# Fourteen up-projection chunks by seven products, the gated product on GpSimd, and another order of sums and lows

## The chip, the cores and the metric

One core of a Trainium2 chip runs the kernel. The metric is the time of one execution in microseconds (us); the figure of a kernel is the median of several runs.

## The reference, cut to what matters

Two transformer layers over a sequence of 512 tokens with 1024 features, in float32. Each layer has an attention part and a gated feed-forward part with a short convolution in it. The change touches only the feed-forward part, and in it the up-projection:

```python
D_MODEL, SEQ, D_FF, CONV_W = 1024, 512, 2816, 3

def conv_ffn(xn, w_up, cw, cb, w_down):
    a = xn @ w_up                                   # (512, 1024) x (1024, 5632)
    ap = jnp.pad(a, ((0, 0), (CONV_W - 1, 0), (0, 0)))
    a = sum(ap[:, j:j + T] * cw[j] for j in range(CONV_W)) + cb
    gate, val = jnp.split(a, 2, axis=-1)
    return (jax.nn.gelu(gate, approximate=True) * val) @ w_down
...
for l in range(2):
    h = h + rms_norm(mix, g[1])                     # mix: the layer's attention
    f = conv_ffn(rms_norm(h, g[2]), w_up[l], conv_w[l], conv_b[l], w_down[l])
    h = h + rms_norm(f, g[3])
```

## The kernel before

**Precision.** Every float32 operand is split into a high part (its value rounded to the matmul's float32r format) and a low part (the rest). A product of two operands is three matmuls: high by high, high by low, low by high (`mm3`, lines 276 to 279). So each weight needs a high, which ScalarE makes with a copy, and a low. A low is made in one of two ways: VectorE subtracts the high from the raw weight, or ScalarE writes the negated high (`scale=-1.0`) and a DMA from GpSimd's queue adds the raw weight to it (`accum_op=ALU.add`).

**Chunks.** The 5632 columns of the up-projection are computed in 22 chunks per layer. Chunk c holds 128 columns of the gate (bank 0 of PSUM) and 128 columns of the value (bank 1), transposed: 128 features by 512 tokens. A chunk takes one of two ways:

- A *plain* chunk: for each of the two banks, 8 blocks of the 1024 features, 3 matmuls each of 512 tokens: 48 matmuls.
- A chunk *by seven products* (Strassen's scheme in Winograd's form; the chunks in the tuple `SEVEN`): the features are halved, the tokens are halved, the two banks are the other pair of halves. Seven products of 4 blocks by 3 matmuls of 256 tokens: 84 matmuls. The seven are named in the code by their weights, A11, S2, S3, A12, S1, A22, S4. The weights' sums S1 to S4 are computed anew for each chunk; the sums of the inputs are there from the start (`XA`, `XB`).

**Order of a chunk by seven.** TensorE runs A11, S2, S3, A12, S1, A22, S4. A11 of the next chunk is opened ahead of S4 of this one (`open_seven`), and ScalarE copies its sum aside (line 1015, `s1`). The results go to quarters of the two banks: `o1` (A11 and A12) and `o2` (S2, S1, S4) share bank 0, `o3` (S3, A22) and `o4` share bank 1. Between the products VectorE makes short sums of 256 columns: `s12` (line 995, behind S2), `s17` (996, behind S3), `o4` (1012), `o3` (1020), and last `o2` (1022, behind S4).

**The work on a finished chunk** is done while the next chunk runs. `taps` does the convolution: ScalarE scales the bank into `bb` (641), VectorE adds the two other taps (642, 644), for the gate and the value. `glu` is ScalarE's GELU (662). `product`, called one chunk later, sends the previous gated product to memory by a DMA from GpSimd's queue (`hD`, 657) and multiplies gate and value (`hc`, 659). The down-projection reads `hD`.

**The weights ahead.** The program order is written out by hand: every engine runs its instructions in the order in which the code names them, and the framework adds the waits. `prepare(c, part)` is called three times in chunk c and drives three generators through `step`, for the chunks c + 1 and c + 2:

- `first_weights` takes the two raw blocks (A11 with A12, A21 with A22), makes high and low of A11 and A12 (706 to 708, low by an adding DMA), S3 and S2 (`sa`, 709 and 711) with `a21 + a22` (710) on the way, their high (712) and low (716), and the sum S4 (714).
- `other_weights` makes high and low of S1 and S4 (725, 728) and of A22 (726, 729).
- `plain_weights` makes highs and lows of a plain chunk, for all but the last two chunks with adding DMAs (`high_added`, lines 53 to 88).

The raw weights come from HBM by SyncE's queue. All of this shares 16 large, 10 middle and 8 small buffers in SBUF and the 8 banks of PSUM.

Of the kernel before, what the change touches and what calls it, by code (L numbers as in the profile page):

```python
# [9 lines left out]
F32 = mybir.dt.float32  # L10
# [14 lines left out]
BIG = 3.0e38  # L25


SEVEN = (5, 6, 8, 9, 11, 12, 14, 15, 17, 18)
ND = NF // 2
LAST = 3  # L30
FILL = 26
# [70 lines left out]
def trunk_kernel(ctx, tc, x, norm_gains, w_qkv_a, w_o_a, w_q_b, w_o_b, kv_norm, w_kvf, b_f,  # L102
# [11 lines left out]
    def t8(shape, dt=F32, name="t8"):  # L114
        return p8.tile(shape, dt, tag="t8", name=name)
# [516 lines left out]
    def ffn(l, bd, cp, nxt, ahead):  # L632
# [19 lines left out]
        def product():  # L652

            if gated:
                c, bb = gated.pop()
                if c - 1 in hc:
                    pool.dma_start(hD[c - 1], hc.pop(c - 1))
                hc[c] = t2([128, T], name="hc")
                dve.tensor_tensor(hc[c], bb[:, 0, :], bb[:, 1, :], ALU.mult)

        def glu(c, bb):
            act.activation(bb[:, 0, :], bb[:, 0, :], AF.Gelu_apprx_tanh)
# [37 lines left out]
        def first_weights(c):  # L700

            r0, r1 = W.take(2)
            w0, w1 = (t8([128, 2, 1024], F32R, name="w") for _ in range(2))
            sa, sb = (t4([128, 1024], name="wsum") for _ in range(2))
            a11, a12, a21, a22 = r0[:, 0:512], r0[:, 512:1024], r1[:, 0:512], r1[:, 512:1024]
            act.copy(w0[:, 0], r0)
            act.activation(w0[:, 1], r0, AF.Copy, scale=-1.0)
            pool.dma_start(w0[:, 1], r0, accum_op=ALU.add)
            dve.tensor_tensor(sa[:, 0:512], a11, a21, ALU.subtract)
            dve.tensor_tensor(sb[:, 0:512], a21, a22, ALU.add)  # L710
            dve.tensor_tensor(sa[:, 512:1024], sb[:, 0:512], a11, ALU.subtract)
            act.copy(w1[:, 0], sa)
            yield
            dve.tensor_tensor(sb[:, 512:1024], a12, sa[:, 512:1024], ALU.subtract)
            yield
            dve.tensor_tensor(w1[:, 1], sa, w1[:, 0].bitcast(F32), ALU.subtract)
            half_way[c] = a22, sb
            v = [t.rearrange("p s (q k c) -> p s q k c", q=2, k=4) for t in (w0, w1)]
            halves[c] = dict(A11=v[0][:, :, 0], A12=v[0][:, :, 1], S3=v[1][:, :, 0], S2=v[1][:, :, 1])

        def other_weights(c):

            a22, sb = half_way.pop(c)
            w2, w3 = (t8([128, 2, 1024], F32R, name="w") for _ in range(2))
            act.copy(w2[:, 0], sb)
            act.copy(w3[:, 0, 0:512], a22)
            yield
            dve.tensor_tensor(w2[:, 1], sb, w2[:, 0].bitcast(F32), ALU.subtract)
            dve.tensor_tensor(w3[:, 1, 0:512], a22, w3[:, 0, 0:512].bitcast(F32), ALU.subtract)
            v = [t.rearrange("p s (q k c) -> p s q k c", q=2, k=4) for t in (w2, w3)]  # L730
            halves[c].update(S1=v[0][:, :, 0], S4=v[0][:, :, 1], A22=v[1][:, :, 0])

# [19 lines left out]
        def prepare(c, part):  # L752

            m, n = c + 1, c + 2
            if n >= NF:
                return
            after = c not in SEVEN
            if m in SEVEN:
                if part == 0 and not after:
                    step(1, m)  # L760
                if part == (0 if after else 1) or part == (1 if after else 2):
                    step(2, m)
            if n not in SEVEN:
                step(0, n)
                if part == 0 and n < NF - 2:
                    step(0, n)
            elif part < 2 or m not in SEVEN:
                step(1, n)

        acts, one, two, raws, later2 = {}, {}, {}, {}, {}  # L770
        H = slice(0, 512), slice(512, 1024)
# [196 lines left out]
        def prod(o, w, x, start=False):  # L968
            half_mm(o, w, x[0:2], x[2], start)
# [6 lines left out]
        for c in range(2, NF):  # L976
# [5 lines left out]
            if c in SEVEN:  # L982
                x21, x22 = [(xT[0][i], xT[1][i], s) for i, s in ((1, LO), (1, HI))]
                banks, s1 = opened or open_seven(c)
                was_open = opened is not None
                opened = None
                w = halves.pop(c)
                W.n_get += 2
                o1, o2, o3, o4 = banks[0][:, LO], banks[0][:, HI], banks[1][:, LO], banks[1][:, HI]
                s12, s17 = (t2([128, 256], name="csum") for _ in range(2))  # L990

                def two_sums():
                    if not was_open:
                        act.copy(s1, o1)
                    dve.tensor_tensor(s12, o2, s1, ALU.add)
                    dve.tensor_tensor(s17, o3, s1, ALU.add)

                prod(o2, w["S2"], (*XB, HI))
                prod(o3, w["S3"], (*XA, HI), True)
                product()  # L1000
                if was_open:
                    two_sums()
                    bb = taps(*before)
                else:
                    bb = taps(*before, two_sums)
                prepare(c, 0)
                glu(before[0], bb)
                prod(o1, w["A12"], x21)
                prod(o2, w["S1"], (*XA, LO))
                prod(o3, w["A22"], (*XB, LO))  # L1010
                prepare(c, 1)
                dve.tensor_tensor(o4, o2, s17, ALU.add)
                if c + 1 in SEVEN:
                    opened = open_seven(c + 1)
                    act.copy(opened[1], opened[0][0][:, LO])
                else:
                    begun = W.get(), bank([128, T], name="up")
                    up(*begun, range(4))
                prod(o2, w["S4"], x22)
                dve.tensor_tensor(o3, o3, s12, ALU.add)  # L1020
                prepare(c, 2)
                dve.tensor_tensor(o2, o2, s1, ALU.add)  # L1022
            else:
                banks = [bank([128, T], name="up") for _ in range(2)]
                for s in range(2):
                    if s == 0 and begun:
                        w, banks[0] = begun
                        up(*begun, range(4, KD))
                        begun = None
                    else:  # L1030
                        up(W.get(), banks[s], range(KD))
                    if c == NF - 2:
                        next(sums)
                    if s == 0 and before:
                        post(*before, (lambda: pair_lows(0)) if c == NF - 1 else None)
                        if c >= NF - 2:
                            pair_highs(c - NF + 2)
                            pair_sums(c - NF + 3)
                    if s == 0:
                        prepare(c, 0)  # L1040
                    prepare(c, 1 + s)
                    next(extra, None)
# [866 lines left out]
```

## Time and profile before

| | before |
|---|---|
| median of 3 runs | 1109.95 us (1109.84 to 1110.57) |
| the profiled execution | 1110.27 us, of it span 1108.5 |
| TensorE busy | 1098.4 us (99%) |
| VectorE busy | 896.6 us (81%) |
| ScalarE busy | 660.2 us (60%) |
| GpSimd busy | 222.2 us (20%) |
| TensorE's granted clock in the stretch 238 to 384 us | 1.00 |

In the rows of the profile PE is TensorE (PEld its weight loads), DVE VectorE, ACT ScalarE, POOL GpSimd, SP SyncE; L709 is line 709. A timeline's row has start and duration in us, engine, line, operation, the tiles written and read, and in brackets how long the engine stood idle before and for whom. Tile `up` is a PSUM bank of the up-projection, `wraw` a raw weight, `w` a split one, `wsum` holds sums of weights, `csum` the short sums. The chunks 5 to 18 of the two layers lie at about 238 to 384 us and 821 to 967 us; in the first of these, VectorE is busy 115 of 146 us.

### The profile page before, as it was taken

Reading aid. Unit: us, or ns where it says so; the run is one execution under the profiler, and the core shown is the slowest. Engines: PE = TensorE matmul, PEld = TensorE weight load, DVE = VectorE, ACT = ScalarE, POOL = GpSimd, SP = SyncE. Lnnn points to the kernel's source line nnn. Section 1 sums busy time; section 2 is a strip of 40 time slices with the busy share of each in tenths; the row PEclk is TensorE's granted clock in tenths of the full one; section 3 lists DMA queues with packets and bytes.
Section 4 is the critical chain, followed back from the end, with each engine's and each line's share of the span. In section 5 each row is a group of like instructions: output and inputs, shape, how many; then the busy total and the mean of one; then the engine's idle time right before and its main releaser. Section 6 shows DMA issues by size and latency. Waiting matters only on the chain.

```text
span 1108.5 us, 18139 instructions
## 1 busy us (share of the span) xinstructions
PE 1098.4 (99%) x6611; PEld 948.4 (86%) x6611; DVE 896.6 (81%) x1494; ACT 660.2 (60%) x1092; POOL 222.2 (20%) x329
## 2 busy tenths in 40 slices
PE   9999999999999999999999999999999999999997
PEld 6988889889999988888888787789989999988886
DVE  6577878978887799997877777858978887799995
ACT  5444566566565547476555677756565565547473
POOL 1832100211111111000010766600211111111000
PEclk9999999999999999999999999999999999999999
DMA  9469864467789989885872677584467779999872
GB/s 325 149 207 408 346 171 132 108 134 196 176 201 216 256 318 341 295 310 108 210 153 76 193 222 211 161 246 124 114 133 191 181 200 219 249 315 340 306 247 77
DMA packets 184563, 237.32 MB, mean 214 GB/s; under 512 B 11737, under 2 KB 131529, under 8 KB 183962
## 3 DMA queue, kind: packets, MB, share of 16 engines
q1 hardware_dynamic: 166970, 176.61, 49.0%
q0 software_dynamic: 17504, 59.55, 23.3%
q8 instruction: 52, 0.85, 0.3%
q14 instruction: 37, 0.30, 0.1%
HBM read 170.28 MB, written 39.63 MB: 189 GB/s over the span
## 4 chain that ended last, share of the span: by engine, by line
PE 89%; DVE 3%; issue 3%; ACT 2%; DMA 2%; POOL 1%; DVEq 0%; POOLq 0%; ACTq 0%
PE up L278 13%; PE up L277 13%; PE up L279 13%; PE acc L278 8%; PE acc L277 8%; PE acc L279 8%; PE qk_ps L278 2%; PE qk_ps L277 2%; PE qk_ps L279 2%; PE first L279 1%; PE first L277 1%; PE first L278 1%; PE o_ps L1762 1%; PE pT_ps L1747 1%; PE v_ps L278 1%
## 5 line engine op out<-in xcount | busy, mean ns | idle before, releaser
L277 PE MATMUL acc<-w 128*128 128x512 f32 (+1 forms) x311 | 120.5, 388 | 0.0
L279 PE MATMUL acc<-w 128*128 128x512 f32 (+1 forms) x311 | 120.4, 387 | 0.0
L57 ACT CAST w<-wraw 128x1024 fp32r<-128x1024 f32 x96 | 99.0, 1048 | 9.5 <-issue 3.9
L278 PE MATMUL acc<-w 128*128 128x512 f32 (+1 forms) x267 | 103.2, 387 | 0.0
L65 DVE TENSOR_TENSOR w<-wraw,w 128x1024 fp32r<-128x1024 f32 x66 | 88.1, 1356 | 15.1 <-ACT w L57 14.7
L641 ACT ACTIVATE bb<-up,conv 128x512 f32<-128x512 f32 x80 | 60.0, 776 | 67.3 <-DVE up L1022 42.8
L278 PE MATMUL up<-xbl,w 128*128 128x512 f32 (+1 forms) x280 | 96.3, 344 | 0.0
L278 PE MATMUL up<-xcl,w 128*128 128x512 f32 (+1 forms) x280 | 96.3, 344 | 0.0
L277 PE MATMUL up<-xch,w 128*128 128x512 f32 (+1 forms) x280 | 96.3, 344 | 0.0
L277 PE MATMUL up<-xbh,w 128*128 128x512 f32 (+1 forms) x280 | 96.3, 344 | 0.0
L279 PE MATMUL up<-xbh,w 128*128 128x512 f32 (+1 forms) x280 | 96.2, 344 | 0.0
L279 PE MATMUL up<-xch,w 128*128 128x512 f32 (+1 forms) x280 | 96.2, 344 | 0.0
L277 PE MATMUL up<-xsh,w 128*128 128x256 f32 x320 | 90.6, 283 | 0.0
L278 PE MATMUL up<-xsl,w 128*128 128x256 f32 x320 | 90.6, 283 | 0.0
L279 PE MATMUL up<-xsh,w 128*128 128x256 f32 x320 | 90.6, 283 | 0.0
L277 PEld LDWEIGHTS acc<-w 128*128 128x128 f32 x311 | 58.4, 188 | 12.0
L279 PEld LDWEIGHTS acc<-w 128*128 128x128 f32 x311 | 58.4, 188 | 11.8
L644 DVE SCALAR_TENSOR_TENSOR bb<-up,conv,bb 128x510 f32<-128x510 f32 x80 | 59.9, 749 | 2.8
L642 DVE SCALAR_TENSOR_TENSOR bb<-up,conv,bb 128x511 f32<-128x511 f32 x80 | 59.4, 742 | 2.6 <-ACT bb L641 2.6
L277 PEld LDWEIGHTS up<-xsh,w 128*128 128x128 f32 x320 | 61.4, 192 | 0.0
L278 PEld LDWEIGHTS up<-xsl,w 128*128 128x128 f32 x320 | 61.4, 192 | 0.0
L279 PEld LDWEIGHTS up<-xsh,w 128*128 128x128 f32 x320 | 61.4, 192 | 0.0
(337 smaller groups left out, 3161.2 us busy)
## 6 DMA issues: line engine op xcount, KB each, us to landing
wraw<-in_w_up_dram SPq DMA_DIRECT2D x88, 512.0 KB, 5.0
w<-wraw POOLq DMA_DIRECT2D x50, 512.0 KB, 6.1
dT<-dsums SPq DMA_DIRECT2D x24, 512.0 KB, 6.0
hD<-hc POOLq DMA_DIRECT2D x44, 256.0 KB, 7.6
dact<-hD SPq DMA_DIRECT2D x44, 256.0 KB, 5.2
wraw<-dT SPq DMA_DIRECT2D x22, 512.0 KB, 6.6
wraw<-in_w_down_dram SPq DMA_DIRECT2D x22, 512.0 KB
dsums<-in_w_down_dram SPq DMA_DIRECT2D x18, 512.0 KB, 5.6
```

The lines of the kernel that those rows point to most:

```text
L57: self.nc.scalar.copy(pair[:, 0], raw)
L65: self.nc.vector.tensor_tensor(pair[:, 1], raw, pair[:, 0].bitcast(F32), ALU.subtract)
L277: pe.matmul(o, ah, bh, start=first, stop=False, skip_group_check=shared)
L278: pe.matmul(o, ah, bl, start=False, stop=False, skip_group_check=shared)
L279: pe.matmul(o, al, bh, start=False, stop=last, skip_group_check=shared)
L641: act.activation(bb[:, s, :], ps, AF.Identity, bias=cp[:, 3, ch:ch + 1], scale=cp[:, 2, ch:ch + 1])
L642: dve.scalar_tensor_tensor(bb[:, s, 1:], ps[:, :T - 1], cp[:, 1, ch:ch + 1], bb[:, s, 1:], ALU.mult, ALU.add)
L644: dve.scalar_tensor_tensor(bb[:, s, 2:], ps[:, :T - 2], cp[:, 0, ch:ch + 1], bb[:, s, 2:], ALU.mult, ALU.add)
L1747: pe.transpose(o[:, k0 + k, :], p[:, hh, k * 128:(k + 1) * 128], ident)
L1762: pe.matmul(o[64 * hh:64 * hh + 64, i * 128:(i + 1) * 128], Vt[hd // 8][:, k, (hd % 8) * 64:(hd % 8) * 64 + 64], pT[j, i, hh][:, k, :], st ...
```

## The change

In both layers:

1. `SEVEN` takes in chunks 7, 10, 13 and 16. Before, one plain chunk stood between each two by seven products; after, chunks 5 to 18 all go by seven products. Chunks 0 to 4 and 19 to 21 stay plain.
2. The gated product (line 659) moves from VectorE to GpSimd, which also issues the DMA of `hD` ahead of it. This holds for all 22 chunks.
3. The low of A22 (line 729, on VectorE) is made by ScalarE's negated copy and an adding DMA in GpSimd's queue, at the head of `other_weights`.
4. The order of sums and lows changes: the first weight sum (709) for chunk c + 2 goes between the two short sums 995 and 996; the low of S3 and S2 (716) of chunk c + 1 goes ahead of them; 710 goes behind the taps, 711 and 714 behind `o4` (1012), which goes ahead of `prepare(c, 1)`. The low of S1 and S4 (728) stays ahead of the last sum (1022).

```diff
-SEVEN = (5, 6, 8, 9, 11, 12, 14, 15, 17, 18)
+SEVEN = (5,6,7,8,9,10,11,12,13,14,15,16,17,18)
...
                 hc[c] = t2([128, T], name="hc")
-                dve.tensor_tensor(hc[c], bb[:, 0, :], bb[:, 1, :], ALU.mult)
+                pool.tensor_tensor(hc[c], bb[:, 0, :], bb[:, 1, :], ALU.mult)
...
             a11, a12, a21, a22 = r0[:, 0:512], r0[:, 512:1024], r1[:, 0:512], r1[:, 512:1024]
+            dve.tensor_tensor(sa[:, 0:512], a11, a21, ALU.subtract)
+            yield
             act.copy(w0[:, 0], r0)
             act.activation(w0[:, 1], r0, AF.Copy, scale=-1.0)
             pool.dma_start(w0[:, 1], r0, accum_op=ALU.add)
-            dve.tensor_tensor(sa[:, 0:512], a11, a21, ALU.subtract)
             dve.tensor_tensor(sb[:, 0:512], a21, a22, ALU.add)
+            yield
             dve.tensor_tensor(sa[:, 512:1024], sb[:, 0:512], a11, ALU.subtract)
             act.copy(w1[:, 0], sa)
-            yield
             dve.tensor_tensor(sb[:, 512:1024], a12, sa[:, 512:1024], ALU.subtract)
             yield
...
             w2, w3 = (t8([128, 2, 1024], F32R, name="w") for _ in range(2))
+            act.copy(w3[:, 0, 0:512], a22)
+            act.activation(w3[:, 1, 0:512], a22, AF.Copy, scale=-1.0)
+            pool.dma_start(w3[:, 1, 0:512], a22, accum_op=ALU.add)
+            yield
             act.copy(w2[:, 0], sb)
-            act.copy(w3[:, 0, 0:512], a22)
             yield
             dve.tensor_tensor(w2[:, 1], sb, w2[:, 0].bitcast(F32), ALU.subtract)
-            dve.tensor_tensor(w3[:, 1, 0:512], a22, w3[:, 0, 0:512].bitcast(F32), ALU.subtract)
...
             if m in SEVEN:
-                if part == 0 and not after:
-                    step(1, m)
-                if part == (0 if after else 1) or part == (1 if after else 2):
-                    step(2, m)
+                step(2, m)
...
-            elif part < 2 or m not in SEVEN:
+            elif part < 2 or after or m not in SEVEN:
                 step(1, n)
+                if after and part == 0:
+                    step(1, n)
...
                     dve.tensor_tensor(s12, o2, s1, ALU.add)
+                    if c + 2 in SEVEN:
+                        step(1, c + 2)
                     dve.tensor_tensor(s17, o3, s1, ALU.add)
...
                 product()
+                if c + 1 in SEVEN:
+                    step(1, c + 1)
...
                 prod(o3, w["A22"], (*XB, LO))
+                dve.tensor_tensor(o4, o2, s17, ALU.add)
                 prepare(c, 1)
-                dve.tensor_tensor(o4, o2, s17, ALU.add)
```

## The prediction

> **What bounds the kernel now.** I read the page first: the busy shares, then the chain that ended last.
>
> ```profile
> span 1108.5 us, 18139 instructions
> PE 1098.4 (99%) x6611; PEld 948.4 (86%) x6611; DVE 896.6 (81%) x1494; ACT 660.2 (60%) x1092; POOL 222.2 (20%) x329
> PE 89%; DVE 3%; issue 3%; ACT 2%; DMA 2%; POOL 1%; DVEq 0%; POOLq 0%; ACTq 0%
> ```
>
> TensorE is busy 99% of the span and carries 89% of the chain: time is won only where matmuls go and lost only where a matmul waits. The profiled execution took 1110.27 us (1.8 of it outside the span); the median of the runs, 1109.95, is 0.3 less. Next the timeline of TensorE in the first layer's up-projections (columns: start, duration, engine).
>
> ```profile
> 227.28 0.39 PE L277 MATMUL up<-xbh,w 128*128 128x512 f32 x1
> 238.16 0.28 PE L277 MATMUL up<-xbh,w 128*128 128x256 f32 x1
> 246.79 0.28 PE L277 MATMUL up<-xbh,w 128*128 128x256 f32 x1
> 248.23 0.28 PE L277 MATMUL up<-xbh,w 128*128 128x256 f32 x1
> ```
>
> Durations overlap, so I take distances between starts. From 227.28 to 238.16 lie the 48 matmuls of a plain chunk: 10.88 us. From 238.16 to 248.23 lie seven products of 12 matmuls: 10.07, or 1.44 each. Product A22 of chunk 5 ends at 246.79, A11 of chunk 6 at 248.23; TensorE waits nowhere in between. The other engines in chunks 5 to 8:
>
> ```profile
> 246.99 0.43 DVE L1012 TENSOR_TENSOR up<-up,csum 128x256 f32<-128x256 f32 x1 [1.32 <-PE up L279]
> 247.80 1.22 DVE L728 TENSOR_TENSOR w<-wsum,w 128x1024 fp32r<-128x1024 f32 x1
> 248.93 0.69 DVE L729 TENSOR_TENSOR w<-wraw,w 128x512 fp32r<-128x512 f32 x1
> 249.87 0.43 DVE L1022 TENSOR_TENSOR up<-up,csum 128x256 f32<-128x256 f32 x1 [0.26 <-PE up L279]
> 250.21 0.68 DVE L659 TENSOR_TENSOR hc<-bb 128x512 f32<-128x512 f32 x1
> 253.09 0.74 DVE L642 SCALAR_TENSOR_TENSOR bb<-up,conv,bb 128x511 f32<-128x511 f32 x1
> 255.98 0.68 DVE L709 TENSOR_TENSOR wsum<-wraw 128x512 f32<-128x512 f32 x1
> 256.57 0.68 DVE L710 TENSOR_TENSOR wsum<-wraw 128x512 f32<-128x512 f32 x1
> 257.29 0.69 DVE L711 TENSOR_TENSOR wsum<-wsum,wraw 128x512 f32<-128x512 f32 x1
> 258.02 0.69 DVE L714 TENSOR_TENSOR wsum<-wraw,wsum 128x512 f32<-128x512 f32 x1
> 258.63 0.43 DVE L1012 TENSOR_TENSOR up<-up,csum 128x256 f32<-128x256 f32 x1
> 248.43 0.37 ACT L1015 COPY csum<-up 128x256 f32<-128x256 f32 x1 [0.39 <-PE up L279]
> 250.34 1.45 ACT L641 ACTIVATE bb<-up,conv 128x512 f32<-128x512 f32 x2 [1.54 <-DVE up L1022]
> 251.68 1.04 ACT L706 CAST w<-wraw 128x1024 fp32r<-128x1024 f32 x1
> 252.62 1.06 ACT L707 ACTIVATE w<-wraw 128x1024 fp32r<-128x1024 f32 x1
> 258.07 1.06 ACT L712 CAST w<-wsum 128x1024 fp32r<-128x1024 f32 x1 [4.40 <-DVE wsum L711]
> 259.03 0.63 ACT L662 ACTIVATE bb<-bb 128x512 f32<-128x512 f32 x1
> 265.63 0.61 ACT L726 CAST w<-wraw 128x512 fp32r<-128x512 f32 x1
> 266.15 1.05 ACT L706 CAST w<-wraw 128x1024 fp32r<-128x1024 f32 x1
> 253.97 0.84 POOL L708 DMA_DIRECT2D w<-wraw  x1 [6.18 <-ACT w L707]
> 254.51 0.87 POOL L657 DMA_DIRECT2D hD<-hc  x1
> ```
>
> What to see: L1012 writes the high half of a bank and starts 0.20 after A22 has finished with its low half (246.79), though S1, which it reads, ended 1.44 before; a bank is handed over whole. VectorE's distances are 0.60 for 512 columns (0.72 where the next needs the result), 1.13 for 1024 (247.80 to 248.93), 0.34 for 256 (249.87 to 250.21), 2.89 for four taps (253.09 to 255.98).
>
> **The change part by part.** *Chunks 7, 10, 13, 16 by seven products:* in two layers this takes 8 x (10.88 - 10.07) = 6.5 us from TensorE, and that is all that can be won.
>
> *Product to GpSimd, low of A22 to a DMA.* A chunk by seven products costs VectorE 2.89 for taps, 1.70 for five short sums, 2.66 for four weight sums (0.60 + 0.72 + 0.73 + 0.61), 2.26 for two lows, and now also 0.60 for the product and 0.60 for A22's low: 10.7, over the 10.07 of TensorE. Where plain chunks stand between, this averages out; 14 in a row without the two removals would lose 0.6 each. With them 9.5 is left. ScalarE gains a pass of 512 columns, 0.52 (265.63 to 266.15), and stays near 7 us; GpSimd has three DMA issues and a product, about 3 us. The new DMA is issued a chunk ahead of A22; its landing is hidden by 10 us of matmuls. By busy time everything fits.
>
> *By order it is tighter.* GpSimd's product is a new neighbour of VectorE's two-input instructions. The nearest rows, and the rows that time the hand-overs:
>
> ```profile
> 192.26 4.62 POOL L676 TENSOR_TENSOR xsum<-xbh,xbl 128x2048 f32<-128x2048 f32 x1 [52.06 <-DVE xbl L349]
> 192.92 5.04 DVE L65 TENSOR_TENSOR w<-wraw,w 128x1024 fp32r<-128x1024 f32 x1
> 24.17 0.46 POOL L1093 TENSOR_TENSOR tu<-qk,rope 128x128 f32<-128x128 f32 x1 [21.99 <-ACT qk L1087]
> 638.93 0.90 POOL L82 DMA_DIRECT2D w<-wraw  x1 [1.41 <-ACT w L59]
> 639.54 1.15 POOL L1696 TENSOR_SCALAR bias<-ck,cq 128x128 f32<-128x128 f32 x2
> L708 POOLq EVENT_SEMAPHORE  x38: 17/43/5618, 213.7 to 930.2; - x38
> 527.42 0.59 ACT L1414 COPY vp<-v_ps 128x512 f32<-128x512 f32 x1
> 528.06 0.19 PEld L277 LDWEIGHTS v_ps<-w,xkh 128*128 128x128 f32 x1 [0.56 <-ACT vp L1414]
> ```
>
> L65 takes 1.22 at its size (as L728), here 5.04: it stood still until 192.92 + 5.04 - 1.22 = 196.74, 0.14 before L676 ended at 196.88. So a GpSimd instruction with two SBUF inputs shuts out a VectorE instruction that also has two. A product of 512 columns lies between L1093 and L676: 0.46 + 384 x (4.62 - 0.46)/1920 = 1.29, and it shuts VectorE out for 1.15. Sums and lows (L709 to L728) are of the kind that is shut out; the short sums and taps read PSUM.
>
> When does the product run? Its place in GpSimd's queue is behind the two added DMAs of the chunk before. Follow one ring, from the sum that ends a chunk (L1022) to the next: L1022 ends, tap 0.04 later (250.30 to 250.34); two taps 1.34; the two passes of A22, 1.04, now ahead of L706; L706 0.94; L707 and the hand-over to L708 1.35; to the issue of hD 0.54; to the product 0.61 (638.93 to 639.54); VectorE shut out for 1.15; then the second S-sum (L711) 0.73, L714 0.61, L1020 0.34, low of S1 and S4 1.13, L1022 itself 0.43. Together 10.25, and 0.04 for a semaphore instruction ahead of the product: 10.29. TensorE is not in this ring, and it is longer than 10.07.
>
> Where does TensorE meet it? Counted from the start of S2, A22 ends at 7.20, L1012 starts at 7.40, and L711 could at 7.74; shut out, it starts at about 8.1. Behind L711 come L712 (257.29 to 258.07: 0.78), the copy of A11's sum (0.96 later, as 258.07 to 259.03), its 0.37, and 0.05 to the weight load (528.01 to 528.06): 2.16. The copy reads the bank in which S2 of the next chunk writes, so S2 waits: from 7.74 it would come at 9.90, in time; from 8.1 it comes at 10.3. So each chunk c for which c + 2 is also one of the seven (5 to 16) takes 10.29 instead of 10.07: 24 x 0.22 = 5.3 us given back. For the first of each run, where the bank is opened late, I add an estimated 0.2, twice. At the end of the loop the products shut out the first lows of the down-projection, whose cover of about 1 us I take as enough.
>
> Sum: -6.5 + 5.3 + 0.4 = -0.8 against 1110.27, so 1109.5 in a profiled execution and about 1109.2 as a median. Bounds of the unknown: the product's hold could be 0.55 (the 0.68 of VectorE's L659 less the 0.14) or 2 x 1.15; the first removes the loss, the second is 24 x 1.15 = 28 more. I stay with 1.15, interpolated between two GpSimd rows of the same kind.
>
> The Trainium skill ("SBUF — State Buffer", section "Who interferes with whom", with "SBUF: two separate sides") says that the pair of ports which VectorE and GpSimd share is held for the full instruction. By that rule the hold is 1.29, 24 x 0.14 = 3.4 us more, and the result 1112.6; the trace shows 0.14 less than the full instruction, and I follow the trace.
>
> **The rivals.** *A: the ring is shorter than it looks, TensorE stays the bound.* Below 10.07 nothing is lost: 1109.95 - 6.5 + 0.4 = 1103.8. For it: every term was taken in other surroundings, and 0.2 in 10.29 is little. Against: two independent counts agree. The other one goes through TensorE: S2 and S3 2.88, hand-over 0.20, L996 0.34, taps 2.89, L710 0.60 (the product can't enter while it runs), hold 1.15, then 2.16: 10.22. Anything below 10.23 is faster by over 0.2% (2.2 us, about what a measurement of this kernel can tell from no change).
>
> *B: slower, by GpSimd's queue.* If the product must wait until the hD issue has run for its whole 0.87 (254.51) instead of 0.61, or an issue is slower beside VectorE, the ring is 0.26 longer: 10.55, and 24 x 0.26 = 6.2 more: 1115.4. It decides from a ring of 10.41 on. For it: the product is the third of three instructions in a queue that has no slack in this ring. Against: 638.93 to 639.54. The Trainium skill's same page ("SBUF: two separate sides") names such a mechanism: GpSimd cannot write a DMA's descriptors while VectorE holds the shared pair. Beside the 1.22 of L716 an issue keeps its length here:
>
> ```profile
> 275.53 1.22 DVE L716 TENSOR_TENSOR w<-wsum,w 128x1024 fp32r<-128x1024 f32 x1
> 275.55 0.85 POOL L82 DMA_DIRECT2D w<-wraw  x1 [5.67 <-ACT w L59]
> ```
>
> By that rule hD's issue would wait for L710 and the ring be up to 0.6 longer, 24 x 0.6 = 14 us: 1123; I give it 3 of B's hundredths.
>
> *C: the change doesn't do what it says.* VectorE is freed of 0.60 for the product but shut out by it for up to 1.15; if the hold fell in full, its 9.5 would be 10.65, and 24 x 0.58 = 14 us lost, 1117. It has an idle stretch of 0.5 before L1012, in which the hold begins, so I count this within B.
>
> **How the numbers follow.** Forecast (ring of 10.23 to 10.41): 0.44; A: 0.28; B with C: 0.28. The forecast's own span is within 0.2%, but it lies nearer to the lower edge (0.06 of ring) than to the upper (0.12), so 0.05 of it goes to faster: faster 0.33, same 0.39, slower 0.28. The range takes in A, down to the full 6.5 (1103.4), below which nothing leads, and B's first price; longer rings are left out.
>
> **What would show it.** Right: in chunks 7, 10, 13 and 16 the 48 matmuls of 512 columns gone for 84 of 256; the start of S2 idle by 0.1 to 0.3 in 12 chunks a layer, released by ScalarE's L1015; L711 lengthened to about 1.0 with the GpSimd product beside it. A: TensorE without waits, L711 at 0.69. B: product later than 0.6 behind hD's issue, S2 waiting 0.4 or more. Wrong in kind: TensorE waiting elsewhere, at A12 for the short sum L995 or for the new DMA.

## The result, and the profile after

| | before | after |
|---|---|---|
| median | 1110.03 us (1109.84 to 1110.57, 4 runs) | 1116.87 us (1116.44 to 1117.17, 4 runs) |
| the profiled execution | 1110.27, of it span 1108.5 | 1116.95, of it span 1115.2 |
| VectorE busy | 896.6 us | 944.4 us |
| GpSimd busy | 222.2 us | 298.7 us |

After is slower by 0.6%: the ratio is 1.0061, 95% interval 1.0048 to 1.0073. The forecast was 1109.2 and no change; the range ended at 1115.4, 1.5 us short of the result. The head of the page and its chain:

```profile
span 1115.2 us, 18998 instructions
PE 1098.0 (98%) x6899; PEld 957.9 (86%) x6899; DVE 944.4 (85%) x1518; ACT 679.7 (61%) x1136; POOL 298.7 (27%) x393
PE 86%; issue 4%; ACT 4%; DVE 3%; DMA 2%; POOL 0%; DVEq 0%; SPq 0%; ACTq 0%; POOLq 0%
```

TensorE carries 86% of the chain where it had 89, ScalarE 4% where it had 2. Which wait that is, the view of the waits says (engine, tile and line, whom it waited for: us in total, times, longest), for the matmuls and for the weight loads:

```profile
PE up L277 <- ACT csum L1021: 7.3, 24, 0.7
PEld up L277 <- ACT csum L1021: 12.2, 24, 0.9
```

S2 waits in 12 chunks of each layer for ScalarE's copy of the sum of A11 (L1021, before L1015). From S2 to S2 lie 10.61 us in the middle of the run, not TensorE's 10.07: 24 x 0.54 = 13.0, less the 6.5 that the seven products save, makes +6.5; the spans differ by 6.7. One turn of the ring in the timeline of after (rows of three engines, in the order of the ring; L711 runs beside hD's issue):

```profile
304.52 1.45 ACT L641 ACTIVATE bb<-up,conv 128x512 f32<-128x512 f32 x2 [1.23 <-DVE up L1028]
305.86 0.62 ACT L726 CAST w<-wraw 128x512 fp32r<-128x512 f32 x1
306.90 1.04 ACT L708 CAST w<-wraw 128x1024 fp32r<-128x1024 f32 x1
307.84 1.06 ACT L709 ACTIVATE w<-wraw 128x1024 fp32r<-128x1024 f32 x1
309.20 0.86 POOL L710 DMA_DIRECT2D w<-wraw  x1 [1.03 <-ACT w L709]
309.74 0.89 POOL L657 DMA_DIRECT2D hD<-hc  x1
310.32 1.62 POOL L659 TENSOR_TENSOR hc<-bb 128x512 f32<-128x512 f32 x1
309.80 0.68 DVE L711 TENSOR_TENSOR wsum<-wraw 128x512 f32<-128x512 f32 x1
311.18 1.32 DVE L713 TENSOR_TENSOR wsum<-wsum,wraw 128x512 f32<-128x512 f32 x1
312.54 0.69 DVE L715 TENSOR_TENSOR wsum<-wraw,wsum 128x512 f32<-128x512 f32 x1
313.48 1.22 DVE L732 TENSOR_TENSOR w<-wsum,w 128x1024 fp32r<-128x1024 f32 x1
314.61 0.43 DVE L1028 TENSOR_TENSOR up<-up,csum 128x256 f32<-128x256 f32 x1
315.13 1.45 ACT L641 ACTIVATE bb<-up,conv 128x512 f32<-128x512 f32 x2 [1.24 <-DVE up L1028]
```

From tap to tap: 315.13 - 304.52 = 10.61. (L713 is the second sum, the prediction's L711; L1028 its L1022.) L713 needs nothing of the product, yet takes 1.32 instead of 0.69: less its own 0.69 its end, 312.50, is 311.81, 0.13 before the product ends at 311.94. The one row that differs from the forecast is the product itself:

```profile
L659 POOL TENSOR_TENSOR hc<-bb x44: 1285/1622/1646, 203.7 to 1011.1; 128x512 f32<-128x512 f32 x44
```

(Shortest, median and longest in ns.) The forecast had 1.29, which is the shortest: the product alone. In the ring its record lasts 1.62, because it begins 0.58 behind the beginning of hD's issue, while that issue ends only at 310.63; from there to 311.94 lie 1.31. So the product does its work behind the issue, and its record begins 0.31 before that. Two turns in the second layer, in which the issue came at another time, show the same:

```profile
895.05 0.69 POOL L657 DMA_DIRECT2D hD<-hc  x1
895.64 1.43 POOL L659 TENSOR_TENSOR hc<-bb 128x512 f32<-128x512 f32 x1
906.15 0.58 POOL L657 DMA_DIRECT2D hD<-hc  x1 [0.36 <-issue]
906.74 1.31 POOL L659 TENSOR_TENSOR hc<-bb 128x512 f32<-128x512 f32 x1
```

Where the issue reaches 0.10 into the product's record, the record lasts 1.43; where it doesn't, 1.31.

There is a second way to a long product. The first one of the layer has nothing in front of it in its queue for 6.81 us and yet lasts 1.65:

```profile
202.96 1.22 DVE L678 TENSOR_TENSOR xsum<-xsum 128x1024 f32<-128x1024 f32 x1
203.68 1.65 POOL L659 TENSOR_TENSOR hc<-bb 128x512 f32<-128x512 f32 x1 [6.81 <-ACT bb L662]
```

L678 has two SBUF operands and runs until 204.18, 0.50 into the product: if this hold too ends 0.14 before the record does, it reaches 0.36 into it, and 0.36 + 1.29 = 1.65. The hold works in both directions. In the ring of after this is not what lengthens the product: L711 ends at 310.48, only 0.16 into its record.

### The profile page after: what moved, and what is told of

The parts are those of the page before. It is cut to its first block, busy times and chain, and to the rows that moved or that the text cites. A ratio compares the mean times of both kernels' runs of the same rounds, so it can differ in the third digit from the quotient of the medians.

```text
span 1115.2 us, 18998 instructions
## 1 busy us (share of the span) xinstructions
PE 1098.0 (98%) x6899; PEld 957.9 (86%) x6899; DVE 944.4 (85%) x1518; ACT 679.7 (61%) x1136; POOL 298.7 (27%) x393
## 4 chain that ended last, share of the span: by engine, by line
PE 86%; issue 4%; ACT 4%; DVE 3%; DMA 2%; POOL 0%; DVEq 0%; SPq 0%; ACTq 0%; POOLq 0%
PE up L277 12%; PE up L279 11%; PE up L278 11%; PE acc L278 8%; PE acc L277 8%; PE acc L279 8%; PE qk_ps L278 2%; PE qk_ps L277 2%; PE qk_ps L279 2%; PE o_ps L1768 1%; PE s_ps L1721 1%; PE q_ps L277 1%; PE first L279 1%; PE first L277 1%; PE first L278 1%
## 5 line engine op out<-in xcount | busy, mean ns | idle before, releaser
L277 PE MATMUL up<-xsh,w 128*128 128x256 f32 x448 | 129.2, 288 | 7.3 <-ACT csum L1021 7.3
L278 PE MATMUL up<-xsl,w 128*128 128x256 f32 x448 | 126.7, 283 | 0.0
L279 PE MATMUL up<-xsh,w 128*128 128x256 f32 x448 | 126.7, 283 | 0.0
L277 PEld LDWEIGHTS up<-xsh,w 128*128 128x128 f32 x448 | 85.7, 191 | 12.2 <-ACT csum L1021 12.2
L279 PEld LDWEIGHTS up<-xsh,w 128*128 128x128 f32 x448 | 85.8, 191 | 0.0
L278 PEld LDWEIGHTS up<-xsl,w 128*128 128x128 f32 x448 | 85.8, 191 | 0.0
L277 PE MATMUL up<-xch,w 128*128 128x256 f32 (+1 forms) x264 | 85.0, 322 | 0.0
L278 PE MATMUL up<-xbl,w 128*128 128x256 f32 (+1 forms) x264 | 84.9, 322 | 0.0
L278 PE MATMUL up<-xcl,w 128*128 128x256 f32 (+1 forms) x264 | 84.9, 322 | 0.0
L277 PE MATMUL up<-xbh,w 128*128 128x256 f32 (+1 forms) x264 | 84.9, 322 | 0.0
L279 PE MATMUL up<-xbh,w 128*128 128x256 f32 (+1 forms) x264 | 84.8, 321 | 0.0
L279 PE MATMUL up<-xch,w 128*128 128x256 f32 (+1 forms) x264 | 84.8, 321 | 0.0
L659 POOL TENSOR_TENSOR hc<-bb 128x512 f32<-128x512 f32 x44 | 67.6, 1537 | 24.3 <-ACT bb L662 13.6
L728 POOL DMA_DIRECT2D w<-wraw x28 | 24.2, 864 | 168.7 <-ACT w L727 168.7
```

The costliest lines, as they stand in the source:

```text
L277: pe.matmul(o, ah, bh, start=first, stop=False, skip_group_check=shared)
L278: pe.matmul(o, ah, bl, start=False, stop=False, skip_group_check=shared)
L279: pe.matmul(o, al, bh, start=False, stop=last, skip_group_check=shared)
L659: pool.tensor_tensor(hc[c], bb[:, 0, :], bb[:, 1, :], ALU.mult)
L728: pool.dma_start(w3[:, 1, 0:512], a22, accum_op=ALU.add)
```

## The experiments

The theory, T: a ring through ScalarE's passes, GpSimd's queue, the hold and VectorE's sums lasts 10.61 us, and S2 is only where TensorE meets it. Its rivals: R, the copy's place on ScalarE; V, VectorE has too much to do; Q, the order in GpSimd's queue doesn't matter. All times below are medians, the ratio is to the kernel before; the distance is that from last sum to last sum in the middle of the run.

**One link at a time.** First the product back on VectorE:

```diff
-                pool.tensor_tensor(hc[c], bb[:, 0, :], bb[:, 1, :], ALU.mult)
+                dve.tensor_tensor(hc[c], bb[:, 0, :], bb[:, 1, :], ALU.mult)
```

> The gated product goes back to VectorE; the DMA of hD stays on GpSimd, all else as after. Theory T (S2 waits because of a ring ScalarE, GpSimd's queue, product, VectorE shut out, second sum, that lasts 10.6 us against TensorE's 10.07): without the product on GpSimd the second sum (L713) takes its bare 0.69 us, ScalarE's copy L1021 comes early enough and S2 waits no more; VectorE has then some 10.1 to 10.4 us of work a chunk, so most of the loss but not all of it goes: 1105 to 1112 us, waits if any at A12 for a short sum. Rival V (VectorE has simply too much to do in a row of 14 such chunks, the product's place makes no difference): giving it 0.6 us more a chunk costs 24 x 0.6 = 14 us: 1118 us or more. Rival R (the place of the copy behind the pass L714 on ScalarE alone makes S2 wait): L713 without the lengthening still leaves the copy behind L714; nothing changes by more than 2 us, 1115 to 1118.

1108.28 us, ratio 0.9982 (0.9973 to 0.9990), distance 10.29. S2 waits no more, 8.6 us of the change go away with this one line, and V, which wanted 1118, falls: VectorE has 0.6 more to do in a chunk, and the time is shorter. What is left over 10.07 goes with the product's new place, ahead of the taps: in the timeline the first tap waits for it, 0.58 longer than for the last sum.

Next ScalarE's copy ahead of the high of S3 and S2:

```diff
-            act.copy(w1[:, 0], sa)
             dve.tensor_tensor(sb[:, 512:1024], a12, sa[:, 512:1024], ALU.subtract)
             yield
+            act.copy(w1[:, 0], sa)
+            yield
...
                     act.copy(opened[1], opened[0][0][:, LO])
+                    if c + 2 in SEVEN:
+                        step(1, c + 2)
```

> On ScalarE the copy of A11's sum (L1021) goes ahead of the pass that makes the high of S3 and S2 (L714); nothing else moves. Rival R (S2 waits only because that copy stands behind L714): the wait of 24 x 0.54 = 13 us goes, and with it all that was given back: about 1104 us. Theory T (the ring of 10.6 us does not run through this copy; S2 is only where TensorE meets it): the wait at S2 goes, and the same 0.5 us a chunk comes up at another product (A12, for the short sum L997), so the time stays: 1115 to 1118 us, with the distance between chunks still 10.5 to 10.6 us. Rival V (VectorE full): also no change.

1116.57 us, ratio 1.0057 (1.0044 to 1.0069), distance 10.62. The wait at S2 is gone and stands at A12, for the short sum (L1000 is after's L997):

```profile
PE up L277 <- DVE csum L1000: 7.0, 24, 0.7
```

The same 24 times, the same 0.7: a wait that is taken away where the ring is met comes up where it is met next. R falls.

Then hD's issue behind the product:

```diff
-                if c - 1 in hc:
-                    pool.dma_start(hD[c - 1], hc.pop(c - 1))
                 hc[c] = t2([128, T], name="hc")
                 pool.tensor_tensor(hc[c], bb[:, 0, :], bb[:, 1, :], ALU.mult)
+                if c - 1 in hc:
+                    pool.dma_start(hD[c - 1], hc.pop(c - 1))
```

> GpSimd multiplies first and issues hD's DMA after it. Theory T with the queue served one after the other (adding DMA 0.86 us, hD 0.54, product 1.31): the ring loses the 0.54 of hD's issue, 10.61 becomes about 10.1 to 10.35, and 24 x 0.26 to 0.5 = 6 to 12 us come back: 1105 to 1111 us. Rival Q (only the hold counts: the product starts when VectorE lets it, whatever stands ahead of it in the queue): no change, 1116 to 1118 us, L713 still 1.32 at the same place. Rival V (VectorE full): no change.

1108.73 us, ratio 0.9986 (0.9977 to 0.9994), distance 10.29. The order of two instructions of GpSimd is worth 8.1 us; Q falls. In its timeline (L657 is now the product):

```profile
307.03 0.86 POOL L710 DMA_DIRECT2D w<-wraw  x1 [1.03 <-ACT w L709]
307.86 1.60 POOL L657 TENSOR_TENSOR hc<-bb 128x512 f32<-128x512 f32 x1
307.63 0.69 DVE L711 TENSOR_TENSOR wsum<-wraw 128x512 f32<-128x512 f32 x1
309.01 1.00 DVE L713 TENSOR_TENSOR wsum<-wsum,wraw 128x512 f32<-128x512 f32 x1
```

The product ends 2.43 after the adding DMA begins, in after 2.74, and L713 is held for 0.31 instead of 0.63. The ring is 10.29, the very length of the forecast, and the time is within 0.5 us of the forecast, but that is chance. The queue gave 0.54 back, and the ring became shorter by 0.32 only: the product stands now just behind the adding DMA's issue, which reaches 0.03 into its record, and lasts 1.60 all the same, since L711 runs until 308.32 (0.46 less 0.14 is 0.32, and 0.32 + 1.29 = 1.61). What the product waits for here is VectorE and no longer the queue.

Last, the hold alone: the same place in the queue, but one operand; the kernel leaves out the multiplication by the value.

```diff
-                pool.tensor_tensor(hc[c], bb[:, 0, :], bb[:, 1, :], ALU.mult)
+                pool.tensor_scalar(hc[c], bb[:, 0, :], 0.5, None, ALU.mult)
```

> GpSimd's instruction reads one SBUF operand instead of two: half the gate instead of gate times value (so the multiplication by the value is left out); its place in the queue stays. If the last link of the ring is that two-input work on GpSimd shuts VectorE's second sum out, L713 takes 0.69 us, S2 waits no more and the time is 1103 to 1105 us, whatever the queue does. If GpSimd shuts VectorE out with one input too, L713 stays lengthened by as much as the instruction allows: with about the same duration 1115 to 1118 us. If the link is a wait for the product's buffer or data and no hold at all: unchanged, 1115 to 1118 us.

1103.40 us, ratio 0.9939 (0.9927 to 0.9952), distance 10.08, TensorE without waits. The instruction lasts longer than the product did, and the queue ahead of it is the same:

```profile
307.48 1.91 POOL L659 TENSOR_SCALAR hc<-bb 128x512 f32<-128x512 f32 x1
307.04 0.99 DVE L711 TENSOR_TENSOR wsum<-wraw 128x512 f32<-128x512 f32 x1
308.42 0.68 DVE L713 TENSOR_TENSOR wsum<-wsum,wraw 128x512 f32<-128x512 f32 x1
```

L713 runs its 0.68 in the middle of those 1.91. So the last link is the hold: where the second sum keeps its bare length, nothing else in the ring is too long. One operand is not free of a hold everywhere: L711, which began 0.44 before, was lengthened by 0.31, and the low L732 at 369.97, which began 0.05 behind the instruction, took 1.97 instead of 1.22. Which part of such an instruction shuts VectorE out stays open.

**Out of the queue's end.** The product was put into GpSimd's queue ahead of the 512 KB adding DMA, first with the buffers as they are, then with one more of the middle size:

```diff
             if m in SEVEN:
                 step(2, m)
+            if part == 0 and not after:
+                product()
...
                 prod(o3, w["S3"], (*XA, HI), True)
-                product()
```

> In the chunks by seven the product and hD's issue go into GpSimd's queue ahead of the 512 KB adding DMA, so that the product can run while VectorE makes the taps, which read PSUM. Theory T (what costs is that the product stands in GpSimd's queue behind that DMA, and so falls on the second sum, which has two SBUF inputs): the product runs beside the taps, L713 takes 0.69 us, the ring falls under TensorE's 10.07, no product waits: 1103 to 1105 us, 6 us faster than before. Rival V (VectorE full): unchanged or worse, 1116 us or more. Rival P (the taps are shut out too, since they have one SBUF input and write to SBUF): taps lengthen from 0.7 to 1.3 or more once a chunk, and the time stays between 1108 and 1118 us.

> The last experiment again (product and hD's issue ahead of the 512 KB adding DMA in GpSimd's queue), but with 11 middle buffers instead of 10 and 6 small ones instead of 8. In that run the first tap waited until the low L717 had read the sum whose buffer the tap's tile takes, and L711 waited for the product, whose buffer it takes; with one buffer more neither is so. Theory T (queue and hold make the ring): the product runs beside the taps, the ring is under TensorE's 10.07, no product of TensorE waits, 1103 to 1105 us. Rival P (the taps are shut out by the product as well): taps of 1.3 us or more, 1108 to 1118 us. Rival V (VectorE full): 1116 us or more.

Both came out slower than after: 1122.31 us, ratio 1.0108 (1.0092 to 1.0123), and 1119.05 us, ratio 1.0081 (1.0067 to 1.0095). L713 was at its bare 0.68 in both, as T has it; the loss is elsewhere. In the first, buffers pass on in the order in which the code is done with them, and with the product later in that order a tap's tile takes the sum that L717 reads, and L711's tile takes the product's:

```profile
306.13 1.45 ACT L641 ACTIVATE bb<-up,conv 128x512 f32<-128x512 f32 x2 [2.30 <-DVE w L717]
311.70 0.69 DVE L711 TENSOR_TENSOR wsum<-wraw 128x512 f32<-128x512 f32 x1 [1.33 <-POOL hc L659]
```

In the second these two are gone, but the first sum L706 now takes the buffer that the adding DMA L710 reads, and L710 stands behind the product (its issue, and of all its issues shortest, median and longest time to landing):

```profile
308.91 1.21 POOL L710 DMA_DIRECT2D w<-wraw  x1
DMA to landing us min/median/max: 4.6/7.4/8.9
317.86 1.92 DVE L706 TENSOR_TENSOR wsum<-wraw 128x512 f32<-128x512 f32 x1 [2.82 <-issue]
```

308.91 + 8.9 = 317.81: L706 starts when the slowest landing is done. (That the landing is what it waits for is read from the buffers and this sum; the row names no releaser.) What the second did show: a product of 1.64 (307.66) beside two taps that kept 0.74 and 0.75. In the first the product ran behind the taps, beside no two-input work of VectorE, and lasted 1.62 behind hD's issue as well (310.05).

**Half a product** on GpSimd, the other 256 columns on VectorE in its idle stretch, with hD's issue ahead and then behind:

```diff
+                second_half()
                 dve.tensor_tensor(o4, o2, s17, ALU.add)
...
-                pool.tensor_tensor(hc[c], bb[:, 0, :], bb[:, 1, :], ALU.mult)
+                pool.tensor_tensor(hc[c][:, LO], bb[:, 0, LO], bb[:, 1, LO], ALU.mult)
+
+        def second_half():
+            c, bb = gated[0]
+            if c not in hc:
+                hc[c] = t2([128, T], name="hc")
+                dve.tensor_tensor(hc[c][:, HI], bb[:, 0, HI], bb[:, 1, HI], ALU.mult)
```

> Half the dose: GpSimd multiplies 256 of the 512 columns, VectorE the other 256 in its idle stretch ahead of L1017's sum; order of the queues as after. If the ring is the GpSimd queue plus the hold, the product's real 1.31 us become about 0.75 and the ring of 10.61 about 10.05, just under TensorE's 10.07: 1103.5 to 1106 us. If the hold is the same for any size (a fixed cost of handing over), little changes: 1114 to 1118 us. If VectorE is simply full, 0.34 more a chunk makes it slower: over 1117 us.

> The same half product with hD's issue behind it: both cuts of the ring together, 10.61 - 0.32 (what the order alone won) - 0.56 = 9.7, well under 10.07. TensorE is the bound again: 1103 to 1104.5 us, and no gain over the half alone beyond what that one still waits. If the two cuts are of the same thing and don't add, the time is that of the better of them.

Neither reached what was expected: 1118.50 us, ratio 1.0076 (1.0064 to 1.0089), distance 10.72, and 1109.87 us, ratio 0.9996 (0.9987 to 1.0005), distance 10.34. The half itself did as expected (1.06 instead of 1.62), so the hold is not a fixed cost, but VectorE's half is two-input work too, and it stands ahead of the sums. In the first of the two:

```profile
310.65 1.06 POOL L659 TENSOR_TENSOR hc<-bb 128x256 f32<-128x256 f32 x1
310.67 1.34 DVE L665 TENSOR_TENSOR hc<-bb 128x256 f32<-128x256 f32 x1
```

1.34 for 256 columns: the half stood still where L713 had stood, and everything behind it with it. The edit put back into the ring what it took out. In the second run L665 still takes 0.96 beside a half product of 1.05 (307.95).

**The parts of the change.** After with the old `SEVEN`, the same with the product on VectorE, and before's code with the new `SEVEN` alone:

```diff
-SEVEN = (5,6,7,8,9,10,11,12,13,14,15,16,17,18)
+SEVEN = (5, 6, 8, 9, 11, 12, 14, 15, 17, 18)
```

> Everything of the change but its first part: SEVEN is as before, with a plain chunk between each two by seven products. My prediction held that a plain chunk between gives the ring time to recover, and that only 14 in a row cost: then the time is that of before, 1108.5 to 1111.5 us, no waits at S2 (few chunks c have both c + 1 and c + 2 by seven). Rival O (the other order of sums costs something even then, because the short sum that A12 needs now stands behind the low L717 in VectorE's queue and the chunk behind a plain one is started late): 1112 to 1117 us, with waits of A12 for L997.

> The run with the old SEVEN (1133.2 us), with the product back on VectorE. If it lost 23 us because the product shuts out the lows that open a run of chunks by seven (L732 took 3.17 us there, ahead of the short sum that A12 waits for), about 1.35 us of each wait goes: 1112 to 1122 us. If the order of sums alone is at fault, hardly anything goes: 1130 us or more.

> Only the first part of the change: before's code with all of chunks 5 to 18 by seven products. My prediction counted 10.7 us of VectorE's work a chunk by distances, 0.6 over TensorE's 10.07: 24 x 0.6 - 6.5 = +8, so 1118 us. Rival O (the old order needs the plain chunk to catch up: there the distance between last sums is 11.38 inside a pair and 19.70 across the plain chunk, and in a row of 14 TensorE's S4 waits for L1012 behind sums that wait in turn for TensorE): at least 24 x 1.31 - 6.5 = +25, 1135 us, and up to 1175 us if both queues wait for each other.

1133.23 us, ratio 1.0203 (1.0187 to 1.0218); 1114.32, ratio 1.0038 (1.0025 to 1.0052); 1181.95, ratio 1.0649 (1.0635 to 1.0664). The first and the last are above what either theory had. With plain chunks between, parts 2 to 4 cost 23 us, and some 19 of these go when the product is back on VectorE. The rows of the first of the three:

```profile
303.18 1.63 POOL L659 TENSOR_TENSOR hc<-bb 128x512 f32<-128x512 f32 x1
302.72 3.17 DVE L732 TENSOR_TENSOR w<-wsum,w 128x1024 fp32r<-128x1024 f32 x1 [0.54 <-ACT w L730]
PE up L277 <- DVE csum L997: 15.5, 8, 3.3
```

In the first chunk of a pair a low of 1.22 is shut out in full, until 302.72 + 3.17 - 1.22 = 304.67, and A12 waits behind it for L997. The plain chunk does not heal this: with it every third chunk opens a run, and the wait comes in 8 of the 10 pairs. The last of the three says what parts 2 to 4 are for: without them TensorE waits 24 times for the short sum L1012, the distance is 13.66, and 14 in a row cost 72 us.

```profile
PE up L277 <- DVE up L1012: 39.7, 24, 1.8
```

The waits are only half of it. From 10.07 to 13.66 are 3.59 us a chunk; a wait takes 1.7 to 1.9 of them. The rest is the clock behind each wait, in the view by stretches (us, then busy us of PE, PEld, DVE, ACT and POOL with their counts, granted clock, DMA share, GB/s; the wait ends at 302.85):

```profile
301.00:303.00 2.00, 0.22 (x2) 0.15 (x2) 1.90 (x4) 1.19 (x2) 0.00 (x0) 1.00 0.17 64
303.00:307.00 4.00, 4.00 (x21) 3.96 (x22) 2.90 (x5) 2.50 (x5) 0.00 (x0) 0.57 0.03 9
307.00:311.00 4.00, 4.00 (x36) 4.00 (x35) 2.50 (x6) 2.95 (x4) 0.75 (x2) 1.00 0.95 257
```

4 us at a granted clock of 0.57 cost 1.7. Over the whole span the clock is 0.971, before's 0.998: of 1181 us an estimated 32. In the run with the old `SEVEN` it is 0.992, an estimated 7 of its 23 us.

**The version without the ring.** The 512 KB DMA first in the queue, then the product, hD, A22's DMA, with ScalarE's passes in that order; a21 + a22 ahead of the taps; the first tap's pass named early and 11 middle buffers for 6 small ones, so that every tile takes a buffer that is long free (the product ahead of hD's issue, as above, is not shown again):

```diff
+            early = part == 0 and not after
-            if m in SEVEN:
+            if m in SEVEN and not early:
                 step(2, m)
...
+            if early:
+                product()
+                if m in SEVEN:
+                    step(2, m)
...
             dve.tensor_tensor(sa[:, 0:512], a11, a21, ALU.subtract)
+            dve.tensor_tensor(sb[:, 0:512], a21, a22, ALU.add)
             yield
```

> All that the runs showed put together, on the code of after: in GpSimd's queue the 512 KB adding DMA first, then the product, then hD's issue, then A22's adding DMA, with ScalarE's passes in the same order; a21 + a22 ahead of the second short sum, the first tap's pass named ahead of the low of S3 and S2, 11 middle and 6 small buffers, so that no tile takes a buffer that is read late. The product then runs beside the taps, which were not lengthened by it (0.74 us beside a product of 1.64 in the run with 11 buffers), and no two-input instruction of VectorE stands in its way. Theory T: no wait at S2, distance between chunks 10.07 to 10.1, 1103 to 1105 us, 6 us faster than before. Rival W (some other wait comes up, at the raw weights, whose loads now start behind the third sum, or at A12): 1106 to 1112 us. Rival V (VectorE full without the hold as well): over 1112 us.

1112.93 us, ratio 1.0025 (1.0013 to 1.0036), as expected in the middle and not at the end: the distance was 10.08 through the run of chunks, but in the last of them A22's DMA, now behind two DMAs of plain weights, came late. The wait in the first layer (in the second it was 2.0 us), and the view by stretches:

```profile
PEld up L279 <- DMA w<-wraw: 3.2, 1, 3.2
370.00:380.00 10.00, 6.96 (x58) 6.76 (x57) 4.48 (x8) 3.95 (x5) 3.96 (x5) 1.00 1.06 268
380.00:385.00 5.00, 5.00 (x21) 4.17 (x21) 3.02 (x4) 0.00 (x0) 0.19 (x1) 0.66 1.05 402
385.00:390.00 5.00, 5.00 (x30) 4.34 (x29) 2.06 (x4) 1.49 (x3) 0.00 (x0) 1.00 1.04 392
```

The wait of 3.2 us is followed by 5 us at a granted clock of 0.66, 1.7 more by the clock. With the old order for that end alone:

```diff
-            early = part == 0 and not after
+            early = part == 0 and not after and n in SEVEN
             if m in SEVEN and not early:
                 step(2, m)
+            if part == 0 and not after and not early:
+                product()
```

> The last kernel, with the old order at the end of the run of chunks alone: where chunk c + 2 is no longer by seven products, A22's passes and its adding DMA go first again, and the product behind them. In the last run 3.2 us of TensorE a layer were lost in chunk 18, where A22 waited for that DMA, and some 1.7 more at the lower clock that followed (granted 0.66 in the 5 us after it). Theory T (queue and hold together were all that ate the gain): both go, and the time is 1103 to 1104.5 us, the 6.5 of the first part of the change in full. Rival W (the end of the run is short of DMA time, whatever the order): the wait moves to the next weight and 1107 us or more remain.

1104.79 us, ratio 0.9951 (0.9937 to 0.9964): faster than both kernels, by 5.5 us than before and by 12 than after, with the whole of the reference's work. In its timeline:

```profile
305.12 1.62 POOL L662 TENSOR_TENSOR hc<-bb 128x512 f32<-128x512 f32 x1
305.16 0.74 DVE L647 SCALAR_TENSOR_TENSOR bb<-up,conv,bb 128x511 f32<-128x511 f32 x1
305.94 0.75 DVE L649 SCALAR_TENSOR_TENSOR bb<-up,conv,bb 128x510 f32<-128x510 f32 x1
307.33 0.43 DVE L1030 TENSOR_TENSOR up<-up,csum 128x256 f32<-128x256 f32 x1 [0.64 <-PE up L279]
307.67 0.68 DVE L718 TENSOR_TENSOR wsum<-wsum,wraw 128x512 f32<-128x512 f32 x1
```

The product lies wholly beside two taps, the sum takes 0.68, and VectorE waits for TensorE (0.64), no longer the other way round.

## Why the prediction was wrong, by its own steps

**The gain of 6.5**, 8 plain chunks at 10.88 less 10.07: right. With the ring out of the way the time was 1103.4 with the multiplication left out and 1104.8 with all of the work; rival A had priced this at 1103.8. Busy time was no obstacle either: in that last kernel VectorE has 0.64 to spare in a chunk. Rival C's price, 1117, is the number that came, but not its way: in after VectorE still stands idle for 0.36 us a chunk, waiting for TensorE ahead of L1017, and with more work on it (the product back) the time was shorter.

**The ring, and where TensorE meets it:** right, down to the instruction. S2 waits for the copy of A11's sum, 12 times a layer, and TensorE is not in the ring.

**The ring's length: this step failed, in one term.** Tap to A22's passes 1.34 as forecast, those passes 1.04, L708 0.94, to the adding DMA 1.36 (1.35), to hD 0.54, to the product 0.58 (0.61), from the end of the hold to L1028's start 2.80 (2.81); the other differences come to 0.02 together, the other way. But "VectorE shut out for 1.15" measured 1.49, from 310.32 to 311.81. The forecast took the product's length of 1.29 from rows where GpSimd had nothing in front, and its place from 0.61 between two recorded starts. Both were read rightly, and they don't add: behind an issue that is still running the record starts early, so 0.58 + 1.62 is to be counted (2.20), or the issue's full 0.89 and then 1.31, not 0.61 + 1.29 (1.90). The 0.3 are the ring's 10.61 less 10.29, 24 x 0.32 = 7.7 us: the whole difference between 1109.2 and 1116.9. That the hold is what makes the ring too long is shown by the run in which the second sum keeps its 0.68 (1103.4) and by the last kernel (1104.8); that the 0.3 come from hD's issue is read from the rows of after. The run with hD's issue behind met the forecast's ring and time by chance, since VectorE's L711 held the product there.

**Rival B** was the case that came: the product that waits for hD's issue, with the ring at 10.55 and 1115.4. It priced 0.26 where 0.32 to 0.34 were due, since it corrected the place and left the length; at 0.28 it had less than the forecast's 0.44. The row that spoke against it, GpSimd's L1696 0.61 behind a DMA, may have had the error in it already: two instructions of 128 columns recorded as 1.15, where L1093 shows 0.46 for one.

**The range's upper end** was B's price and no more. What a ring is too long is paid 24 times: 0.06 us of ring make the 1.5 us by which the end was short, and no term was known that well.

**The Trainium skill** ("SBUF — State Buffer", "Who interferes with whom") gave a hold of the full instruction, 1.29, and 1112.6 by it. The traces show VectorE going on 0.12 to 0.14 before the recorded end in after and in the run with the old `SEVEN`, as the forecast took it; both took 1.29 for the product's length, and so both lacked the same 0.3. The rule that GpSimd can't write a DMA's descriptors while VectorE holds the pair, which had 3 hundredths, should not have been priced: the Trainium skill's page gives it ("SBUF: two separate sides") for VectorE's two-port modes, and says ("Who interferes with whom") that `tensor_tensor`, which the weight sum here is, has none. The trace agrees: hD's issue lasts 0.89 beside L711's 0.68, and 0.89 also where only taps run beside it (309.46, in the first run with the product ahead of the 512 KB DMA).

**Not weighed:** that part 4 could cost or earn by itself. The forecast put 0.2 us on the opening of each run of chunks; with the old `SEVEN`, where every pair opens a run, A12 waited for up to 3.3 us there, and up to 0.9 with the product back on VectorE. And the 10.7 of VectorE's work that the new `SEVEN` would need without the other parts, 8 us slower by the sum, was 72 in the run: TensorE and VectorE waited for each other, and the lower clock behind each wait, which no sum had, cost about as much as the wait.

## What to carry to other kernels

Where a step is put behind other work in a queue, count from the start of what stands right ahead: its whole recorded duration, then the bare duration of the step. A distance between recorded starts and a duration taken elsewhere don't go together. Ask for both directions who shuts out whom. Where a wait moves with the same count and size when it is removed, look for the ring behind it and cut the ring: here the order of two GpSimd instructions was worth 8 us, the place of the waiting copy nothing. Where TensorE waits, look at the granted clock behind the wait too. Before moving a step, see which tile takes its buffer next, since buffers pass on in the order in which the code is done with them.

## What the runs showed of the hardware

- Where a GpSimd product stands behind a DMA issue that is still running, its record begins before its turn and is longer by as much: 1.62 where the issue reaches 0.31 into it, 1.43 at 0.10, 1.31 where the issue has ended, 1.29 with nothing in front.
- GpSimd and VectorE, each with two SBUF operands, shut each other out. VectorE goes on 0.12 to 0.14 before the recorded end of GpSimd's product; the product was held back by VectorE's L678 and lasted 1.65 (203.68). Recorded starts don't tell who wins: a low that had begun 0.46 before the product's record was shut out in full all the same (L732, 3.17 instead of 1.22). Whether the issue of hD that ran then had a part in it is open.
- A GpSimd instruction with one SBUF operand left a sum that began 0.94 into it alone (0.68 within 1.91), but a low that began 0.05 into another took 1.97 instead of 1.22.
- Taps, which read PSUM and one SBUF operand, keep 0.74 beside the product.
- A wait of 3.2 us of TensorE was followed by 5 us at a granted clock of 0.66; waits of 1.8 us, one in each chunk, by 4 us at 0.57 each. In after, with waits of at most 0.9 us in the weight loads, the clock is 1.00 from 821 to 967 us.
